# Merging the last two feature groups of an FFN's second product, and a finishing root from a kept eps / r^2

## The chip, the cores and the metric

The kernel runs on one core of one Trainium2 chip (trn2). The metric is the device time of one launch in microseconds; the kernel before was run three times: 2975.94, 2977.49 and 2983.4 us, median 2977.49. One of these executions was profiled, and all rows below are of that one.

## The reference

One layer of a streaming encoder, for 2048 new frames of one stream (the prompt) and 32 frames of a running stream (the sample), 2080 tokens of width 1024, all in float32:

- mixer: RMSNorm, one input projection, eight heads of stick-breaking attention and eight heads of a Mamba-2 scan, both normalised, one output projection; `h = x + RMSNorm(mixer)`;
- FFN: `gu = RMSNorm(h) @ w_up`, whose two halves of 2816 features are the gate and the up branch; the gate goes through a causal convolution over three frames and a GeLU, is multiplied by up, and the result goes through `w_down` (2816 x 1024); `y = h + RMSNorm(f)`, with f the product of `w_down`.

RMSNorm is `x * rsqrt(mean(x*x) + eps) * g` with eps = 1e-6. Outputs are y, the new keys and values, and the states of the scan and of both convolutions.

## The kernel before, in words

Feature-major: 128 channels stand on the partitions, tokens run along the free dimension. Tokens are worked in four blocks (`SBS`, line 37), numbered 0 to 3: three of 512 tokens and one of 544, which is 512 of the prompt and the 32 of the sample. A block of 544 is computed as two tiles of 272 tokens (`tiles_of`, line 58), since one PSUM bank holds 512 columns; the other blocks are one tile.

Products in full precision are made of three fast ones: every operand is held as a high part and a remainder, and `dense` (line 118) issues hi·hi, hi·lo and lo·hi for each 128 rows of the contraction. So a weight tile holds two parts of up to eight 128 x 128 squares (`weight`, line 98), 1024 KB when full. The split is done once, in block 0: load (L107), high part on ScalarE (L108), remainder on GpSimd (L109), store to DRAM (L112). Later blocks load both parts from there with one DMA (L104). Three such tiles rotate (`WBUFS`, line 21), whatever part of a tile is filled.

**The FFN** is `Tail`. `up` (line 979) computes one group of 128 gate features and the 128 up features that belong to them, and leaves the activation as `ah` and `al` (L1033 on ScalarE, then L1034 on GpSimd); there are 22 such features j. `down` (line 1038) multiplies the activations of one entry of `GROUPS` by their rows of `w_down`: for each pair of the eight output squares c it loads a weight tile, accumulates over the n features of the group in one PSUM tile, and adds it to the running sum `f` in SBUF on VectorE (L1065; the first group copies, L1063). With `end` it also squares f (ScalarE L772) and adds up the squares on GpSimd (L773) for the closing norm. Activations have four buffers (line 893).

**Order of the work.** `stream` (line 1094) is the list of steps of one block after its attention: output projection, residual, norm, then for each feature group the `up`s, and one `down` behind the first `up` of the group after. The steps are drawn as filler between the attention instructions of the block that comes next (`fill`, called from `heads`), three matmuls at a time, and TensorE's order is pinned to that list (`pin`). The last two groups' products are not in the list: they are kept as `self.owed` and run in the stream of the block behind, eight steps of them at once (while the norm of the attention output is made) and the others after the residual. Block 3 has no attention behind it: its stream runs alone (`alone`, line 1143), with three PSUM banks for these products and no pinned order, and its owed products close the kernel. There, and only there, the two tiles of 272 tokens are taken one after the other, each with its own loads of the weights, and `finish` (line 1074) closes tile a's norm, adds h and stores y before tile b's in program order. Where nothing is pinned, instructions are put in order at compile time by a list scheduler that simulates the engines; each engine and the SyncE queue of DMAs then run that order.

**Roots.** `rstd_steps` (line 156) turns a sum of squares into reciprocal roots: small matmuls bring the sums into columns (L166), VectorE scales them (L176 or L179), GpSimd raises to the power -0.5 (L184), small matmuls spread the column over partitions again (L195), ScalarE copies it out (L201). `root` makes r, the reciprocal root of the norm ahead of the FFN. r is not applied to the input of the up branch, so f is too small by that factor, and `finish` makes up for it: it calls `rstd_steps` with `of` = the kept column of r.

Of the kernel before, what the change touches and what calls it, by code (L numbers as in the profile page):

```python
# [8 lines left out]
F32 = mybir.dt.float32  # L9
# [3 lines left out]
ALU = mybir.AluOpType  # L13
# [10 lines left out]
P = 128  # L24
# [9 lines left out]
EPS = 1e-6  # L34
# [23 lines left out]
def tiles_of(n):  # L58
    return [(0, n)] if n <= 512 else [(0, n // 2), (n // 2, n)]


class Kernel:
# [93 lines left out]
    def rstd_steps(self, pool, psp, pt, sq, n, width, tag="rstd", out=None, rcol=None, of=None):  # L156


        nc = self.nc
        nb = (n + P - 1) // P  # L160
        nf, e = divmod(n, P)
        ps = psp.tile([P, 512], F32, name=pt)
        for b in range(nb):
            q = min(P, n - b * P)
            for i, t in enumerate(sq):
                nc.tensor.matmul(  # L166
                    ps[:q, b : b + 1], t[:, b * P : b * P + q], self.ones[:, 0:1],
                    start=i == 0, stop=i == len(sq) - 1,
                )
        v = pool.tile([P, 8], F32, name="rn_v") if rcol is None else rcol  # L170
        if e:
            nc.vector.memset(v[:], 1.0)
        if of is None:
            if e:
                nc.vector.tensor_scalar(v[:e, nf:nb], ps[:e, nf:nb], 1.0 / width, EPS, op0=ALU.mult, op1=ALU.add)
            nc.vector.tensor_scalar(v[:, :nf], ps[:, :nf], 1.0 / width, EPS, op0=ALU.mult, op1=ALU.add)  # L176
        else:
            for rows, cols in ((slice(0, P), slice(0, nf)),) + (((slice(0, e), slice(nf, nb)),) if e else ()):
                nc.vector.scalar_tensor_tensor(  # L179
                    v[rows, cols], ps[rows, cols], 1.0 / width, of[rows, cols], op0=ALU.mult, op1=ALU.mult  # L180
                )
            nc.vector.tensor_tensor(v[:, :nb], v[:, :nb], of[:, :nb], op=ALU.mult)
            nc.vector.tensor_scalar(v[:, :nb], v[:, :nb], EPS, 0.0, op0=ALU.add, op1=ALU.add)
        nc.gpsimd.tensor_tensor(v[:, :nb], v[:, :nb], self.mhalf[:, :nb], op=ALU.pow)  # L184
        if of is not None:
            nc.vector.tensor_tensor(v[:, :nb], v[:, :nb], of[:, :nb], op=ALU.mult)
        yield
        r = pool.tile([P, 544], F32, name=tag) if out is None else out
        ps = psp.tile([P, 512], F32, name=pt)
        for b in range(nb):  # L190
            q = min(P, n - b * P)
            if b == 4:
                nc.scalar.copy(r[:, :512], ps[:])
            c0 = b % 4 * P
            nc.tensor.matmul(  # L195
                ps[:, c0 : c0 + q], v[:, b : b + 1].to_broadcast([P, P]), self.ident[:, :q], start=True, stop=True
            )
        if nb == 5:
            nc.scalar.copy(r[:, 512:n], ps[:, : n - 512])
        else:  # L200
            nc.scalar.copy(r[:, :n], ps[:, :n])  # L201
        self.rcol = v
        yield r
# [676 lines left out]
class Tail:  # L880
# [1 line left out]

    GROUPS = [(3 * i, 3) for i in range(6)] + [(18, 2), (20, 2)]

    def __init__(self, kn, att, ctx, pu):
        self.kn, self.att = kn, att
# [149 lines left out]
    def down(self, s, g, acts, tiles, end=False):  # L1038

        kn, nc, att = self.kn, self.kn.nc, self.att  # L1040
        j0, n = self.GROUPS[g]
        first = tiles[0][0] == 0
# [51 lines left out]
    def stream(self, s, cat):  # L1094
        nt = SBS[s][1]
        a, b = (0, nt // 2), (nt // 2, nt)
        owed, self.owed = self.owed or iter(()), None
        yield from islice(owed, 8)
        yield from self.out_units(s, cat, a)
        chain = self.residual(s, a)  # L1100
        for n, _ in enumerate(self.out_units(s, cat, b)):
            yield
            if n % 4 == 0:
                next(chain, None)
        self.root(s, a)
        for _ in self.residual(s, b):
            pass
        self.split(s, a)
        self.split(s, b)
        self.root(s, b)  # L1110
        yield from owed
        done = iter(())
        if s:
            done = (i for h in (0, SBS[s - 1][1] // 2) for i in self.finish(s - 1, h, h + 256, self.f))
        groups = self.GROUPS
        tiles = tiles_of(nt)
        acts = {}
        for g, (j0, n) in enumerate(groups):
            acts[g] = []
            for j in range(j0, j0 + n):  # L1120
                for i, _ in enumerate(self.up(s, j, acts[g])):
                    yield
                    if j and i % 2:
                        next(done, None)
                if j == j0 and g and g < len(groups) - 1:
                    yield from self.down(s, g - 1, acts.pop(g - 1), tiles)
        g = len(groups) - 1

        def last():
            for t in [tiles] if s < NSB - 1 else [[t] for t in tiles]:  # L1130
                for e in range(2):
                    yield from self.down(s, g - 1 + e, acts[g - 1 + e], t, e == 1)
                if s == NSB - 1:
                    for _ in self.finish(s, *t[0], self.f):
                        pass

        self.owed = last()

    def count(self, s):
# [161 lines left out]
```

## Time and profile before

| | |
|---|---|
| runs | 2975.94, 2977.49, 2983.4 us; median 2977.49 |
| profiled execution | 2975.94 us, of which the span from first to last instruction is 2973.7 us |
| TensorE matmuls | 2832.0 us busy (95% of the span), 16175 |
| VectorE | 1576.6 us (53%) |
| ScalarE | 1238.4 us (42%) |
| GpSimd | 1256.1 us (42%) |
| DMA | 571.58 MB, 192 GB/s over the span |
| chain that ended last | TensorE 76%, VectorE 12%, DMA 5% |
| granted TensorE clock | 0.978 of full speed over the span |

In the rows PE is the matmul engine, PEld its weight loads, DVE VectorE, ACT ScalarE, POOL GpSimd, and SPq the SyncE queue that issues nearly all DMAs. Times are microseconds from the first instruction, unless they are marked ns. Block 0's FFN runs from about 900 to 1400 us, block 3 runs alone from about 2447 us, and the closing products begin at about 2917 us. In a line of the timeline the bracket at the end is the time that the engine sat idle ahead of the instruction, and what ended it.

### The profile page before, as it was taken

Reading aid. Unit: us, or ns where it says so; the run is one execution under the profiler, and the core shown is the slowest. Engines: PE = TensorE matmul, PEld = TensorE weight load, DVE = VectorE, ACT = ScalarE, POOL = GpSimd, SP = SyncE. Lnnn points to the kernel's source line nnn. Section 1 sums busy time; section 2 is a strip of 40 time slices with the busy share of each in tenths; the row PEclk is TensorE's granted clock in tenths of the full one; section 3 lists DMA queues with packets and bytes.
Section 4 is the critical chain, followed back from the end, with each engine's and each line's share of the span. In section 5 each row is a group of like instructions: output and inputs, shape, how many; then the busy total and the mean of one; then the engine's idle time right before and its main releaser. Section 6 shows DMA issues by size and latency. Waiting matters only on the chain.

```text
span 2973.7 us, 43439 instructions
## 1 busy us (share of the span) xinstructions
PE 2832.0 (95%) x16175; PEld 2327.7 (78%) x16175; DVE 1576.6 (53%) x2386; ACT 1238.4 (42%) x2514; POOL 1256.1 (42%) x1077
## 2 busy tenths in 40 slices
PE   8999999989989999999999999999999999999996
PEld 6777778866767777887777777867777779899996
DVE  7676676546664544437544445574545544623334
ACT  4344444346665444436433334653444433311111
POOL 3555555344766665547322223462322325411113
PEclk9999999989999999999999999999999999999998
DMA  5545453657666777876654456646444445655555
GB/s 174 178 149 172 149 165 119 177 147 241 211 237 240 263 242 257 280 256 213 207 178 173 161 183 220 199 163 212 161 162 166 149 173 206 223 183 170 178 177 173
DMA packets 234660, 571.58 MB, mean 192 GB/s; under 512 B 49514, under 2 KB 101362, under 8 KB 205906
## 3 DMA queue, kind: packets, MB, share of 16 engines
q1 hardware_dynamic: 234450, 568.81, 57.4%
q8 instruction: 129, 2.11, 0.3%
q14 instruction: 81, 0.66, 0.1%
HBM read 435.22 MB, written 133.50 MB: 191 GB/s over the span
## 4 chain that ended last, share of the span: by engine, by line
PE 76%; DVE 12%; DMA 5%; ACT 2%; issue 2%; POOL 1%; SPq 1%; DVEq 0%; POOLq 0%; ACTq 0%
PE o L124 37%; PE u L124 12%; PE t L124 11%; PE pa L848 4%; PE z L812 4%; PE pt L833 3%; PE o L365 2%; DVE xc L341 2%; DVE prow L662 1%; DMA w<-wS_out 1%; DVE acB L436 1%; DVE x L263 1%; DVE f L1086 1%; DMA acB<-acD 1%; DVE xc L337 1%
## 5 line engine op out<-in xcount | busy, mean ns | idle before, releaser
L124 PE MATMUL o<-xhi,w 128*128 128x512 f32 (+2 forms) x3968 | 1043.3, 346 | 30.9 <-ACT xhi L287 8.0
L124 PEld LDWEIGHTS o<-xhi,w 128*128 128x128 f32 x3968 | 698.2, 192 | 132.1 <-issue 9.3
L124 PE MATMUL o<-xlo,w 128*128 128x512 f32 (+2 forms) x1984 | 684.1, 345 | 4.8 <-DVE xlo L273 3.6
L109 POOL TENSOR_TENSOR w<-wraw,w 128x1024 fp32r<-128x1024 f32 (+2 forms) x156 | 366.6, 2350 | 247.0 <-ACT w L108 219.7
L667 POOL TENSOR_TENSOR beta<-beta,prow 128x512 f32<-128x512 f32 (+3 forms) x256 | 256.7, 1003 | 449.1 <-DVE prow L662 420.7
L124 PEld LDWEIGHTS o<-xlo,w 128*128 128x128 f32 x1984 | 380.7, 192 | 52.8 <-DVE xlo L273 5.3
L124 PE MATMUL u<-xhi,w 128*128 128x512 f32 x1056 | 350.3, 401 | 2.2 <-ACT rstd L201 2.2
L124 PE MATMUL o<-ah,w 128*128 128x512 f32 x992 | 340.7, 404 | 7.5 <-DVE f L1065 7.5
L662 DVE TENSOR_TENSOR_SCAN prow<-gam,prow,z 128x513 f32<-128x513 f32 x192 | 244.9, 1278 | 174.5 <-ACT beta L660 172.7
L1019 POOL TENSOR_TENSOR y<-y,gb 128x512 f32<-128x512 f32 (+1 forms) x88 | 115.6, 1315 | 495.4 <-ACT gb L1018 492.7
L124 PEld LDWEIGHTS u<-xhi,w 128*128 128x128 f32 x1056 | 200.3, 190 | 56.4 <-issue 4.4
L659 ACT ACTIVATE gam<-z 128x512 f32<-128x512 f32 (+2 forms) x320 | 173.4, 542 | 141.0 <-PE z L812 92.4
L124 PEld LDWEIGHTS o<-ah,w 128*128 128x128 f32 x992 | 187.8, 189 | 52.5 <-DVE f L1065 8.9
L836 ACT COPY wt<-pt 128x512 f32<-128x512 f32 (+3 forms) x282 | 148.1, 530 | 178.4 <-PE pt L833 175.8
L124 PE MATMUL u<-xlo,w 128*128 128x512 f32 x528 | 210.7, 399 | 0.0
L108 ACT CAST w<-wraw 128x1024 fp32r<-128x1024 f32 (+2 forms) x156 | 155.2, 995 | 120.0 <-PE o L124 97.1
L1011 DVE SCALAR_TENSOR_TENSOR y<-gb,cv,y 128x512 f32<-128x512 f32 (+1 forms) x176 | 163.1, 927 | 68.9 <-ACT y L1009 66.1
L124 PE MATMUL o<-al,w 128*128 128x512 f32 x496 | 197.0, 397 | 0.0
L124 PE MATMUL t<-xhi,w 128*128 128x272 f32 x960 | 188.2, 292 | 2.9 <-DVE f L1065 2.8
L833 PE MATMUL pt<-ident,beta 128*128 128x128 f32 x1088 | 180.5, 281 | 8.7 <-DVE rn_v L176 3.8
L833 PEld LDWEIGHTS pt<-ident,beta 128*128 128x128 f32 x1088 | 134.3, 144 | 60.6 <-issue 25.1
L662 DVE TENSOR_TENSOR_SCAN prow<-gam,ones,z 128x129 f32<-128x129 f32 (+3 forms) x128 | 112.1, 877 | 126.1 <-ACT beta L660 119.8
(271 smaller groups left out, 4907.9 us busy)
## 6 DMA issues: line engine op xcount, KB each, us to landing
w<-wS_up SPq DMA_DIRECT2D x132, 1024.0 KB, 4.8
w<-wS_dn SPq DMA_DIRECT2D x72, 768.0 KB, 4.8
wS_up<-w SPq DMA_DIRECT2D x44, 1024.0 KB, 4.8
w<-wS_out SPq DMA_DIRECT2D x39, 1024.0 KB, 6.2
wraw<-wup SPq DMA_DIRECT2D x44, 512.0 KB, 5.8
k<-kS SPq DMA_DIRECT2D x80, 256.0 KB, 3.8
wS_dn<-w SPq DMA_DIRECT2D x24, 768.0 KB, 4.5
w<-wS_dn SPq DMA_DIRECT2D x32, 512.0 KB, 4.0
```

Source lines behind the costliest of these rows:

```text
L108: nc.scalar.copy(hi[:, :n, :], raw[:, :n, :])
L109: nc.gpsimd.tensor_tensor(lo[:, :n, :], raw[:, :n, :], hi[:, :n, :].bitcast(F32), op=ALU.subtract)
L124: mm = nc.tensor.matmul(ps[:, : c1 - c0], l[:, k, :], at(r, k0 + k)[:, c0:c1], start=first and i == 0 and k == 0, stop=last and i == 2 and ...
L659: nc.scalar.activation(g[:, c0:512], z, AF.Sigmoid, scale=-0.125)
L662: nc.vector.tensor_tensor_scan(back(pr), back(g), z[:, 0:1].to_broadcast([P, n + 1]), self.kn.ones[:, 0:1] if prev is None else prev, op0= ...
L667: eng.tensor_tensor(b[:, :n], b[:, :n], pr[:, c0 + 1 : 513], op=ALU.mult)
L812: mm = nc.tensor.matmul(z[:, :n], q[:, P * b : P * b + P], k[:, :n], start=e == 0, stop=e == 1 and kc < s)
L833: mm = nc.tensor.transpose(t[:, P * j : P * j + P], w[:, P * j : P * j + P], kn.ident[:])
L836: copy(wt[:, : n // P, P * b : P * b + P], t[:, :n].rearrange("p (i q) -> p i q", q=P))
L848: nc.tensor.matmul(av[DH * (j % 2) : DH * (j % 2) + DH, c0:], v[:, j, :], wt[:, j, c0:], start=kc == s and j < 2, stop=kc == 0 and j > 1,)
L1011: nc.vector.scalar_tensor_tensor(y[:, :W], gb[:, i : i + W], kn.col(wc + i), y[:, :W], op0=ALU.mult, op1=ALU.add)
L1019: nc.gpsimd.tensor_tensor(y[:, :W], y[:, :W], t, op=ALU.mult)
```

## The change

The last two entries of `GROUPS`, (18, 2) and (20, 2), become one, (18, 4). The owed work is then one call of `down` with four features, with `end` set, instead of two with two features each. In `rstd_steps`, a call with `rcol` now keeps eps / r^2 there (one GpSimd multiply of the column ahead of the power) instead of r; a call with `of` adds that kept column in the one VectorE instruction that scales the sum, and the power is then the result, where before it took a product with r, a second product, an addition of eps, the power and a third product. The working column is always a tile of its own, `rn_v`.

```diff
-        v = pool.tile([P, 8], F32, name="rn_v") if rcol is None else rcol
+        v = pool.tile([P, 8], F32, name="rn_v")
         if e:
             nc.vector.memset(v[:], 1.0)
...
+        for rows, cols in ((slice(0, P), slice(0, nf)),) + (((slice(0, e), slice(nf, nb)),) if e else ()):
+            if of is None:
+                nc.vector.tensor_scalar(
+                    v[rows, cols], ps[rows, cols], 1.0 / width, EPS, op0=ALU.mult, op1=ALU.add
+                )
+            else:
                 nc.vector.scalar_tensor_tensor(
-                    v[rows, cols], ps[rows, cols], 1.0 / width, of[rows, cols], op0=ALU.mult, op1=ALU.mult
+                    v[rows, cols], ps[rows, cols], 1.0 / width, of[rows, cols], op0=ALU.mult, op1=ALU.add
                 )
-            nc.vector.tensor_tensor(v[:, :nb], v[:, :nb], of[:, :nb], op=ALU.mult)
-            nc.vector.tensor_scalar(v[:, :nb], v[:, :nb], EPS, 0.0, op0=ALU.add, op1=ALU.add)
+        if rcol is not None:
+            nc.gpsimd.tensor_scalar(rcol[:, :nb], v[:, :nb], EPS, 0.0, op0=ALU.mult, op1=ALU.add)
         nc.gpsimd.tensor_tensor(v[:, :nb], v[:, :nb], self.mhalf[:, :nb], op=ALU.pow)
-        if of is not None:
-            nc.vector.tensor_tensor(v[:, :nb], v[:, :nb], of[:, :nb], op=ALU.mult)
...
-    GROUPS = [(3 * i, 3) for i in range(6)] + [(18, 2), (20, 2)]
+    GROUPS = [(3 * i, 3) for i in range(6)] + [(18, 4)]
...
-                if j == j0 and g and g < len(groups) - 1:
+                if j == j0 and g:
                     yield from self.down(s, g - 1, acts.pop(g - 1), tiles)
...
             for t in [tiles] if s < NSB - 1 else [[t] for t in tiles]:
-                for e in range(2):
-                    yield from self.down(s, g - 1 + e, acts[g - 1 + e], t, e == 1)
+                yield from self.down(s, g, acts[g], t, True)
```

## Rows read from the trace of the kernel before

**Rows 1.** Busy time and granted clock by stretch; the first line names the columns.
```profile
core 0: us, PE busy (x) PEld busy (x) DVE busy (x) ACT busy (x) POOL busy (x), PEclk, DMA share, GB/s
...
2447.00:2917.00 470.00, 460.98 (x3551) 454.33 (x3546) 184.49 (x388) 110.45 (x243) 123.00 (x119) 0.99 0.56 190
2917.00:2974.00 57.00, 33.95 (x217) 31.88 (x215) 29.62 (x70) 8.75 (x20) 23.12 (x26) 0.78 0.61 188
```

**Rows 2.** TensorE's waits, 2917 to 2974: us in total, times, longest.
```profile
PE t L124 <- DMA w<-wS_dn: 4.3, 4, 2.0
PE t L124 <- DVE f L1065: 3.5, 4, 1.5
```

**Rows 3.** Pieces of the chain that ended last: start, us, what, how many.
```profile
1282.92 0.47 PE u L124 x2
...
2911.07 6.03 PE o L124 x48
2917.09 1.52 PE t L124 x12
```

**Rows 4.** Timeline of SyncE's DMA issues from 2905: start, us, count of issues.
```profile
2905.07 6.55 SPq L104 DMA_DIRECT2D w<-wS_dn  x2
...
2917.12 29.78 SPq L104 DMA_DIRECT2D w<-wS_dn  x14
```

**Rows 5.** DMA issues from 2862: count, KB each, median us to landing.
```profile
w<-wS_dn SPq DMA_DIRECT2D x16, 512.0 KB, 4.6
w<-wS_up SPq DMA_DIRECT2D x6, 1024.0 KB, 4.8
```

**Rows 6.** Two stretches of the end, columns as in Rows 1.
```profile
2935.50:2938.90 3.40, 3.40 (x17) 3.40 (x16) 0.88 (x2) 0.00 (x0) 0.00 (x0) 0.50 0.36 128
...
2949.20:2956.00 6.80, 5.93 (x26) 5.93 (x27) 4.96 (x13) 2.44 (x6) 4.73 (x6) 0.50 0.85 281
```

**Rows 7.** GpSimd timeline: remainder of feature 21, blocks 0 and 3.
```profile
1286.37 1.27 POOL L1034 TENSOR_TENSOR al<-y,ah 128x512 fp32r<-128x512 f32 x1 [2.08 <-ACT ah L1033]
...
2920.76 1.35 POOL L1034 TENSOR_TENSOR al<-y,ah 128x544 fp32r<-128x544 f32 x1 [1.72 <-ACT ah L1033]
```

**Rows 8.** TensorE's waits over the whole span, columns as in Rows 2.
```profile
PE o L124 <- DVE f L1065: 7.5, 5, 2.5
PE t L124 <- DVE f L1065: 6.3, 5, 2.8
PE u L195 <- DVE rn_v L186: 6.3, 5, 2.0
...
PE o L124 <- DMA w<-wS_out: 4.7, 2, 3.8
...
PE u L195 <- POOL rcol L184: 3.1, 2, 1.7
PE z L812 <- DVE rn_v L186: 2.3, 2, 1.2
```

**Rows 9.** VectorE timeline, owed products of block 0.
```profile
1370.10 5.73 DVE L946 SCALAR_TENSOR_TENSOR m<-m,cv,rstd 128x256 f32<-128x256 f32 x8 [1.05 <-ACT rstd L201]
1375.75 0.68 DVE L1065 TENSOR_TENSOR f<-o,f 128x512 f32<-128x512 f32 x1
```

**Rows 10.** VectorE timeline at the last root.
```profile
2959.46 0.21 DVE L179 SCALAR_TENSOR_TENSOR rn_v<-u,rcol 128x2 f32<-128x2 f32 x2 [2.25 <-PE u L166]
2959.71 0.16 DVE L182 TENSOR_TENSOR rn_v<-rn_v,rcol 128x3 f32<-128x3 f32 x1
2959.91 0.17 DVE L183 TENSOR_SCALAR rn_v<-rn_v 128x3 f32<-128x3 f32 x1
2961.12 0.16 DVE L186 TENSOR_TENSOR rn_v<-rn_v,rcol 128x3 f32<-128x3 f32 x1 [1.04 <-POOL rn_v L184]
```

**Rows 11.** TensorE timeline at the last root.
```profile
2958.69 0.74 PE L166 MATMUL u<-ones,fsq 128*128 128x1 f32 x6 [1.95 <-POOL fsq L773]
```

**Rows 12.** GpSimd and VectorE groups by shape: count, busy us, mean ns.
```profile
L109 POOL TENSOR_TENSOR w<-wraw,w 128x512 fp32r<-128x512 f32 x8 | 10.6, 1328 | 0.8 <-ACT w L108 0.8
...
L184 POOL TENSOR_TENSOR rcol<-rcol,mhalf 128x2 f32<-128x2 f32 x6 | 4.8, 799 | 6.8 <-DVE rcol L176 5.7 <-DMA v<-vS 1.1
...
L644 POOL MEMSET gam<- 128x1 f32 x3 | 0.2, 99 | 0.0
```

More of the change, by code (lines that the diff above doesn't have):

```diff
@@ L169, in rstd_steps @@
                 )
-        v = pool.tile([P, 8], F32, name="rn_v") if rcol is None else rcol
+        v = pool.tile([P, 8], F32, name="rn_v")
         if e:
             nc.vector.memset(v[:], 1.0)
[L173 to L178, printed above, removed]
+        for rows, cols in ((slice(0, P), slice(0, nf)),) + (((slice(0, e), slice(nf, nb)),) if e else ()):
[4 more added lines that the diff above has]
+            else:
                 nc.vector.scalar_tensor_tensor(
-                    v[rows, cols], ps[rows, cols], 1.0 / width, of[rows, cols], op0=ALU.mult, op1=ALU.mult
+                    v[rows, cols], ps[rows, cols], 1.0 / width, of[rows, cols], op0=ALU.mult, op1=ALU.add
                 )
-            nc.vector.tensor_tensor(v[:, :nb], v[:, :nb], of[:, :nb], op=ALU.mult)
-            nc.vector.tensor_scalar(v[:, :nb], v[:, :nb], EPS, 0.0, op0=ALU.add, op1=ALU.add)
+        if rcol is not None:
+            nc.gpsimd.tensor_scalar(rcol[:, :nb], v[:, :nb], EPS, 0.0, op0=ALU.mult, op1=ALU.add)
         nc.gpsimd.tensor_tensor(v[:, :nb], v[:, :nb], self.mhalf[:, :nb], op=ALU.pow)
-        if of is not None:
-            nc.vector.tensor_tensor(v[:, :nb], v[:, :nb], of[:, :nb], op=ALU.mult)
         yield
```

## The prediction

> **What bounds the kernel now.** I read the busy times by stretch first. In the 470 us in which block 3 runs alone TensorE is busy 461 us at a granted clock of 0.99, and nothing but fewer matmuls would help there; in the last 57 us it is busy 34 us at 0.78 [rows 1]. The change removes no matmul: the owed products are 8 outputs x 4 features x 3 = 96 matmuls per tile in either form. So it can only give back idle TensorE time, and the place to look is that last stretch. Then TensorE's waits there: 4.3 us for weight loads of w_down, 3.5 us for the additions to f [rows 2]. The pace of TensorE at full clock comes from the chain: 48 matmuls of 272 columns in 6.03 us, 0.1256 us each [rows 3]. At that pace the closing products (two tiles, 192 matmuls) need 24.1 us. They begin at 2917.1 [rows 3] and end at 2958.69 - 1.95 = 2956.74, where the idle time ahead of the last root begins [rows 11]: 39.6 us. With 1.5 us for the twelve small matmuls of tile a's root (twice the 0.74 of rows 11) the floor is 25.6 us, and 14.0 us are lost. Part of that is clock: two stretches of 3.4 and 6.8 us, behind waits of TensorE, show a granted clock of 0.50, that is 1.2 instead of 2.4 GHz [rows 6]; at half speed they lose up to 1.7 + 3.4 us.
>
> **Why the weights come late there.** One load of 512 KB serves 12 matmuls, 1.51 us. Three tiles rotate, and a load takes 4.6 us from issue to landing [rows 5], so a tile comes round in 1.51 + 4.6 = 6.1 us and the three of them give one load each 2.04 us. The queue shows 29.78 / 14 = 2.13 us [rows 4]: it is the round trip that sets the pace, not TensorE's 1.51. In the long stretch ahead, one load serves 48 matmuls, and there is no such wait.
>
> **The change part by part** (own time of the profiled execution: 2975.94 us, span 2973.7 and 2.2 around it; 1.55 below the median of the runs).
>
> 1. *Closing products, tail.* Four features fill the tile: 8 loads of 1024 KB in place of 16 of 512. A full load takes 4.8 us [rows 5] and serves 24 matmuls, 3.01 us; the round trip gives one load each (3.01 + 4.8) / 3 = 2.60 us, under 3.01, so TensorE sets the pace and the waits for weights go, with the half clock behind them. What is late next is feature 21: before, the first pass used features 18 and 19 alone, which were long done; now the first output wants 21, whose remainder lands at 2920.76 + 1.35 = 2922.11 [rows 7], 5.0 us after TensorE is free. Nine matmuls (1.1 us) can go ahead, or 27 (3.4 us) if the scheduler starts three outputs in the three banks: idle 1.6 to 3.9 us, I take 2.5. Evacuations halve too, 8 per tile, 3 banks hold 4.5 us of work; tile a's finish puts eight products on VectorE in one go (as the 5.73 us of [rows 9]), so I leave 0.5 us for f, and 0.5 us for a low clock. New tail 25.6 + 3.5 = 29.1 us, gain 10.5. Best 25.6 + 1.6, gain 12.4; worst 25.6 + 3.9, with the 3.5 of f as now and 3.0 of half clock, gain 3.6.
>
> The Trainium skill speaks against the size of this. Its page "DMA: Bandwidth & Descriptors" (section "Anatomy of one DMA — SWDGE (gpsimd) path") fits about 2.0 us plus bytes / 436e3 per DMA, an estimate of 3.2 us for 512 KB and 4.4 for 1 MB; with 3.2 us the round trip would give a load each 1.57 us, close to TensorE's 1.51, and the loads would explain 1 us of the tail. The rows disagree (4.6 us to landing here, loads 2.13 us apart, from SyncE's queue), so I go by them.
>
> 2. *Last root.* On the path that ends last stand L182, L183 and L186, from 2959.71 to 2960.09 and from 2961.12 to 2961.28 [rows 10], 0.16 + 0.17 + 0.16 us and the hops between them: 0.55 us gone, 0.5 to 0.7.
>
> 3. *Owed products of blocks 0 to 2.* TensorE waits 7.5 + 6.3 us for additions to f, of which 3.5 are the tail's: 10.3 us [rows 2, 8]. They arise where VectorE has eight residual products in a row, 5.73 us, with the addition behind them [rows 9], while two PSUM banks hold 6 matmuls each. With 12 per bank the same block of VectorE time is nearly covered, and 24 additions of 0.68 us fall away. Between 0 and 10.3 I take 6.
>
> 4. *Roots inside finish, blocks 0 to 2.* TensorE waits 6.3 + 2.3 us for L186, less 2.0 at the very end: 6.6 us [rows 8]. Without L186 the power on GpSimd releases TensorE; L186 does not queue behind VectorE's other work any more, but the wait for GpSimd stays. Between 0 and 6.6 I take 2.5.
>
> 5. *Root that keeps eps / r^2.* One more GpSimd instruction ahead of the power, eight times. The trace has no such instruction; between the smallest memset, 0.10 us, and the power itself, 0.80 [rows 12], so -0 to +6.4 in sum, and only two of the roots have TensorE waiting for them (3.1 us in two waits [rows 8]): +0.2 to +1.6, I take +1. The others lie beside up products. The queue behind it on GpSimd is the power and the squares; a shift of under 1 us there is hidden by the same products.
>
> 6. *Feature 21 in blocks 0 to 2, and squares that come earlier.* In block 0 TensorE ends the up product at 1283.39 [rows 3], the remainder ends at 1287.64 [rows 7], 4.25 us later; nine matmuls of 0.235 us cover 2.1. Idle 2.1 us, for what is pinned behind it. Behind it a wait for the output projection's weights follows (3.8 of 4.7 us [rows 8]), and one tile of weights less ahead of it lets that load start sooner: the delay may cost nothing or the wait may shrink. Two outputs now also bring their squares into the stretch in which ScalarE and GpSimd make the norm. For three blocks -3.8 to +6.3, I take +2.
>
> 7. *At nothing:* splitting the weights in block 0 (four GpSimd instructions twice as long in place of eight of 1.33 us [rows 12]; the raw loads are as many bytes) and all stores and loads of blocks 0 to 2, hidden by the products of the same stretch; uncovered, one split of a tile, twice 1.33, is the price.
>
> Sum: -10.5 - 0.55 - 6 - 2.5 + 1 + 2 = -16.55 us: 2975.94 - 16.55 = 2959.4 us, against the median 2959.4 + 1.55 = 2961 us.
>
> **The rivals.**
>
> - *All of it.* Every wait for f and L186 goes and the tail meets its best: -12.4 - 0.7 - 10.3 - 3 + 0.2 = -26.2, 2951 us. For it: the waits are named. Against: a wait that goes is often followed by the next in line. 0.12.
> - *The loads were not the limit.* The 2.13 us are the echo of TensorE's other stops; fuller loads give back the 4.3 us booked to them, and the wait for feature 21 takes 3.5 of it: 1 us is left. Then -1 - 0.55 - 6 - 2.5 + 3 = -7, 2970 us. For it: no more than 4.3 us are booked to the loads [rows 2]. Against: the landing time in rows 5. 0.06. (The page's fit, above, would have it so.)
> - *Given back inside.* The tail gains 7, but the new order of the scheduler moves the waits of parts 3 and 4 elsewhere (0 in sum), and parts 5 and 6 cost 1.4 + 3: -7.5 + 4.4 = -3, 2974 us, no difference. For it: these waits are where VectorE's residual products stand, and those stay. 0.15.
> - *Slower: feature 21.* Place: the first output of the owed products in all four blocks. TensorE stands, and then goes at 1.2 GHz as it does behind the waits of rows 6: 2.1 + 3.4 us in each of blocks 0 to 2, 16.5 us; in the tail 3.9 + 3.4 beside the 3.5 for f and the 4.3 for loads, which a late release of the tiles keeps, 15.1 where 14.0 are lost now, +1. Less 8.5 for parts 3 and 4 and plus 1 for part 5 it is +10, 2987 us. It decides from the point where stalls and low clock together pass the 19 us that parts 1 to 4 give. For it: the order is pinned in blocks 0 to 2. Against: a wait of 2.1 us there fits beside the norm, behind which TensorE waits anyway [rows 8]. 0.04.
>
> **How the numbers follow.** Forecast 0.63, at 2961 us, with 2953 to 2968 as its own range; the rivals as above, 0.37. To 2951 on the fast side and 2972 on the slow side the range takes in the full gain, the loads' rival and part of the third; outside is about 0.2. What a measurement tells from no change is about 0.3%, 8.9 us, so faster means under 2968.6: 0.61 of the forecast, 0.12, and 0.05 from the second and third rivals, 0.78. Slower, over 2986.4: 0.05. The remainder 0.17 is the same.
>
> **What would show it.** In the profile after: eight loads of 1024 KB in the tail, about 3 us apart, no wait of TensorE for them, a clock of 1.00 in most of it, closing products done in some 29 us; right at their start a wait for `al` L1034 of 1.6 to 3.9 us. Additions to f behind the first group fall from 7 x 8 outputs x 5 tiles = 280 to 6 x 8 x 5 = 240, and TensorE's wait for them from 13.8 to under 6 us. L182, L183 and L186 are gone and what TensorE waited for them is partly booked to the power. Wrong: loads still more than 3.2 us apart with TensorE waiting for them (part 1), waits for `al` in the owed products of blocks 0 to 2 of more than 2 us each (part 6), or a sum of waits in 1280 to 2917 that is no smaller (parts 3 and 4).

## The result, and the profile after

The changed kernel was slower, not faster: 2985.38 us (median of 22 runs, 2973.27 to 2988.79) against 2978.97 us for the kernel before (22 runs, 2972.66 to 2989.31); ratio 1.002, 95% interval 1.0011 to 1.0028. Forecast was 2961. The profiled execution took 2988.79 us, the longest of its runs, with a span of 2987.0 us; the profiled one of before stood 3 us under its median. So of the 13.3 us between the two spans about half belongs to the executions, and sizes are taken from medians and ratios, places from the traces.

The end of the kernel, where most was forecast, did what it should. Stretches of the kernel after (answers to [rows 1]; the last one begins with the closing products):

```profile
core 0: us, PE busy (x) PEld busy (x) DVE busy (x) ACT busy (x) POOL busy (x), PEclk, DMA share, GB/s
2447.00:2938.00 491.00, 476.70 (x3610) 466.18 (x3609) 185.89 (x383) 115.13 (x252) 125.67 (x124) 0.98 0.55 187
2938.00:2987.00 49.00, 29.64 (x223) 28.20 (x221) 22.64 (x49) 9.28 (x21) 23.03 (x26) 0.87 0.57 197
```

TensorE's waits of the kernel after from 2938 on (answer to [rows 2]):

```profile
PE u L167 <- POOL fsq L772: 3.0, 1, 3.0
PE t L124 <- DVE f L1064: 1.9, 1, 1.9
PE u L194 <- POOL rn_v L185: 1.3, 1, 1.3
PE t L124 <- ACT ah L1032: 1.1, 1, 1.1
PE t L124 <- POOL al L1033: 0.8, 1, 0.8
```

Its SyncE issues there (answer to [rows 4]) and their landing (answer to [rows 5]):

```profile
2926.80 6.35 SPq L104 DMA_DIRECT2D w<-wS_dn  x2
...
2938.85 18.22 SPq L104 DMA_DIRECT2D w<-wS_dn  x6
```

```profile
w<-wS_dn SPq DMA_DIRECT2D x16, 1024.0 KB, 4.9
```

Six loads in 18.22 us are 3.04 us each: the pace is TensorE's 24 matmuls, 3.01 us, and no wait for weights is left. (The 4.9 us are the median of the sixteen such loads of the whole execution, the eight closing ones among them.) The closing products run from 2938.66, their first matmul, to 2969.24, where the idle time ahead of the last root begins: 30.6 us in place of 39.6. But they begin 21.6 us later than the 2917.09 of [rows 3]. Of these, 5.0 us stand ahead of the first output product's copy (782.0 us before, 787.0 after), in work that the change does not touch. Behind it TensorE's idle time grew. From the last up products of block 0 (1280 us) to those of block 2, first in the trace of before and then after, columns as above:

```profile
1280.00:1830.00 550.00, 535.48 (x2630) 417.37 (x2629) 263.50 (x355) 211.32 (x467) 186.55 (x194) 0.98 0.56 193
1830.00:2447.00 617.00, 602.49 (x3039) 460.60 (x3039) 338.82 (x434) 285.87 (x622) 227.26 (x233) 0.99 0.53 177
```

```profile
1280.00:1830.00 550.00, 532.12 (x2586) 411.53 (x2585) 252.69 (x338) 208.99 (x458) 184.79 (x191) 0.98 0.56 193
1830.00:2447.00 617.00, 602.49 (x3052) 461.66 (x3050) 334.13 (x418) 287.31 (x623) 227.60 (x236) 0.99 0.52 176
```

With block 3 up to its closing products (470.00 - 460.98 in [rows 1], 491.00 - 476.70 above) TensorE stands idle for 38 us before and 47 us after. What it waits for over the whole span (answer to [rows 8]) tells part of where that was lost:

```profile
PE z L811 <- DVE prow L661: 24.5, 18, 3.6
PE u L194 <- POOL rn_v L185: 12.4, 6, 4.2
...
PE o L124 <- DVE y L1027: 7.8, 1, 7.8
...
PE o L124 <- DMA w<-wS_out: 4.1, 1, 4.1
...
PE t L124 <- DVE f L1064: 2.1, 2, 1.9
```

and in the trace of before:

```profile
PE z L812 <- DVE prow L662: 16.5, 14, 3.4
...
PE o L124 <- DVE y L1028: 2.7, 1, 2.7
...
PE u L195 <- POOL rn_v L184: 1.4, 1, 1.4
```

The waits for f are nearly gone (13.8 to 2.7 us, 0.6 of it in a row further down). In their place are longer waits for VectorE's scans of the attention, `prow`, and one wait of 7.8 us for an up product, where before took 2.7. The waits for a root did not go: the 12.4 us for the power on GpSimd stand in place of 10.8 (6.3 and 3.1 in [rows 8], and the 1.4).

### The profile page after: what moved, and what is told of

It reads as the page before. It is cut to its first block, busy times and chain, and to the rows that moved or that the text cites. A ratio compares the mean times of both kernels' runs of the same rounds, so it can differ in the third digit from the quotient of the medians.

```text
span 2987.0 us, 43324 instructions
## 1 busy us (share of the span) xinstructions
PE 2837.6 (95%) x16175; PEld 2326.6 (78%) x16175; DVE 1552.6 (52%) x2322; ACT 1239.8 (42%) x2510; POOL 1253.3 (42%) x1081
## 4 chain that ended last, share of the span: by engine, by line
PE 74%; DVE 13%; DMA 5%; issue 3%; ACT 2%; POOL 2%; SPq 1%; DVEq 0%; POOLq 0%; ACTq 0%
PE o L124 36%; PE u L124 12%; PE t L124 10%; PE pa L847 4%; PE z L811 4%; PE pt L832 3%; PE o L364 2%; DVE xc L340 2%; DVE acB L435 1%; DMA acB<-acD 1%; DVE prow L661 1%; DVE xc L336 1%; DVE x L262 1%; DVE xlo L272 1%; DMA w<-wS_out 1%
## 5 line engine op out<-in xcount | busy, mean ns | idle before, releaser
L124 PEld LDWEIGHTS o<-xhi,w 128*128 128x128 f32 x3968 | 699.0, 192 | 138.6 <-issue 13.7
L109 POOL TENSOR_TENSOR w<-wraw,w 128x1024 fp32r<-128x1024 f32 (+1 forms) x152 | 365.7, 2406 | 246.6 <-ACT w L108 221.2
L108 ACT CAST w<-wraw 128x1024 fp32r<-128x1024 f32 (+1 forms) x152 | 154.4, 1016 | 118.6 <-PE o L124 98.1
```

The lines of the kernel that those rows point to most:

```text
L108: nc.scalar.copy(hi[:, :n, :], raw[:, :n, :])
L109: nc.gpsimd.tensor_tensor(lo[:, :n, :], raw[:, :n, :], hi[:, :n, :].bitcast(F32), op=ALU.subtract)
L124: mm = nc.tensor.matmul(ps[:, : c1 - c0], l[:, k, :], at(r, k0 + k)[:, c0:c1], start=first and i == 0 and k == 0, stop=last and i == 2 and ...
```

## Experiments

Each kernel was compared with the kernel before on the same chip; the medians of before were 2978.2 to 2980.2 us. In the diffs `rstd_steps` is meant where nothing else is said.

**The two halves apart.** Merge alone (`GROUPS` ends in (18, 4), old `rstd_steps`):

> One half of the change: GROUPS ends in (18, 4), the roots are those of the kernel before. The tail should show its gain of about 10 us in any theory (8 loads of 1024 KB, about 30 us from the first closing product to the last). Theory A, the merge in blocks 0 to 2 gives it back, since the fuller owed steps move VectorE's and GpSimd's work between the attention's instructions: middle about +16, sum about +6 us, ratio to before 1.002, and a tail that begins some 15 us later than 2917. Theory B, the root gives it back: the middle stays, tail begins within 4 us of 2917, sum -9 to -10, ratio 0.997. Theory C, each edit moves the order of the middle by itself, some 8 us each: sum about -2, ratio 0.9993.

Measured: 2973.54 us, ratio 0.9981 (0.9970 to 0.9991). Root alone (new `rstd_steps`, old `GROUPS`):

> The other half: the finishing root in one step from eps / r^2, GROUPS as before. The tail keeps its 16 loads of 512 KB and its 39.6 us. Theory A (the merge is what costs): the root gives its 0.5 us at the end and up to 2.5 inside, sum -0.5 to -3 us, ratio 0.999 to 1.000. Theory B (the root is what costs; the added GpSimd instruction, and block 2's closing residual products released earlier, ahead of the up products' evictions): +12 to +16 us, ratio 1.004 to 1.0055, and a wait of some 8 us of TensorE for VectorE's up product near 2585. Theory C (both): +5 to +8, ratio 1.002 to 1.003.

Measured: 2985.79 us, ratio 1.0027 (1.0015 to 1.0040). So it is the root that costs, as theory B has it, against my own first guess; but only in kind: B asked for -9 to -10 us of the merge and at least +12 of the root, and -5.0 and +7.3 were measured. The wait near 2585, which I had put to the root, is in the trace of the merge and not of the root. It is told below.

**The merge in the closing products alone.** Block 0 stores the two halves side by side, blocks 1 and 2 load halves, block 3 the whole (entry g + 1 is a further one, (18, 4)):

```diff
...
-                for e in range(2):
-                    yield from self.down(s, g - 1 + e, acts[g - 1 + e], t, e == 1)
+                if s == NSB - 1:
+                    yield from self.down(s, g + 1, acts[g - 1] + acts[g], t, True)
+                else:
+                    for e in range(2):
+                        yield from self.down(s, g - 1 + e, acts[g - 1 + e], t, e == 1)
...
```

> Only block 3's closing products take four features with one load of 1024 KB; blocks 0 to 2 keep (18, 2) and (20, 2) and their roots. All that stands before 2917 us is then the order of the kernel before. Theories A, B and C agree here: tail -9 to -10 us, nothing elsewhere, ratio 0.9965 to 0.997, about 2969 us. Against them theory D, that the tail's gain is not real but taken from the stretch ahead of it (the fuller loads displace others, the up products of features 20 and 21 come later): the tail shortens and begins later by the same, ratio 1.000.

Measured: 2975.79 us, ratio 0.9989 (0.9976 to 1.0002): less than the 9 us expected, and not told apart from no change. Its trace tells why the end gave less. Up to 2900 us VectorE, ScalarE and GpSimd run exactly the instruction sequences of the kernel before (read off both traces: operation, operands, shapes). From the last activation `ah` to the end it takes 47.4 us where before took 53.7: 6.3 us. The loads and f give back their waits as in the changed kernel, but another grows. TensorE's waits from 2917 on:

```profile
PE u L172 <- POOL fsq L779: 5.4, 1, 5.4
PE u L201 <- DVE rn_v L192: 2.0, 1, 2.0
PE t L130 <- ACT ah L1039: 1.1, 1, 1.1
PE t L130 <- POOL al L1040: 0.8, 1, 0.8
PE t L130 <- DMA w<-wS_dn: 0.3, 1, 0.3
```

The squares of f at the end are late by 5.4 us, where [rows 11] had 1.95. VectorE has tile a's eight residual products in one stretch of 5.0 us (2942.8 to 2947.8) ahead of tile b's last three additions to f. That this stretch makes the squares late is read from the order and not shown by a run; the edit meant to test it (under "A miss") changed no order. With the new root beside the merge (the changed kernel, and the next run) the wait is 3.0, and 1.9 us stand as a wait for f instead.

> The closing products as in the run before this one (four features only in block 3), with the finishing root in one step from eps / r^2 everywhere. Theory A: tail -10, root -0.5 to -3, sum -10 to -13, ratio 0.9957 to 0.9967. Theory B: tail -10, root +12 to +16, sum +2 to +6, ratio 1.001 to 1.002. Theory C: -2 to -5, ratio 0.998 to 0.9993.

Measured: 2983.47 us, ratio 1.0015 (1.0005 to 1.0025): theory B again: the root costs 7.7 us beside this merge, 7.3 alone. Beside the whole merge it is more, 2973.5 to 2985.4.

**Which part of the root.** The kept column made by VectorE straight from the sums:

```diff
-            nc.gpsimd.tensor_scalar(rcol[:, :nb], v[:, :nb], EPS, 0.0, op0=ALU.mult, op1=ALU.add)
+            for rows, cols in ((slice(0, P), slice(0, nf)),) + (((slice(0, e), slice(nf, nb)),) if e else ()):
+                nc.vector.tensor_scalar(
+                    rcol[rows, cols], ps[rows, cols], EPS / width, EPS * EPS, op0=ALU.mult, op1=ALU.add
+                )
```

> GROUPS as before; the finishing root in one step, but eps / r^2 is made by VectorE straight from the sums in PSUM (sum x eps / width + eps^2), so that the power on GpSimd has nothing ahead of it. The new root with the GpSimd instruction cost 8 us by itself. Theory R1, it is the GpSimd instruction ahead of the power, for which TensorE waits: then this is -0.5 to -3 us against before, ratio 0.999 to 1.000. Theory R2, it is the shorter finish, which lets the closing residual products of the block before fall elsewhere between the attention's instructions: then the loss stays, +6 to +9 us, ratio 1.002 to 1.003. Theory R3, it is mere chance of the order and of where the clock falls: anything between.

Measured: 2981.85 us, ratio 1.0011 (0.9997 to 1.0024): between R1 and R2, and told apart neither from no change nor from the root with the GpSimd multiply (1.0015 to 1.0040). Theory R3, chance of the order, is not excluded here. With the merge in the closing products:

> Four features in block 3's closing products alone, and the root of e5_root_dve. Against the same kernel with the GpSimd instruction (2983.5 us) and the one with the old root (2975.8): theory R1, 2973 to 2976 us, ratio 0.998 to 0.999; theory R2, 2981 to 2984, ratio 1.001 to 1.002. In either the last root should be 0.5 to 0.7 us shorter than with the old root.

Measured: 2974.73 us, ratio 0.9979 (0.9967 to 0.9991), as R1 has it, and clear of the 1.0015 (1.0005 to 1.0025) with the GpSimd multiply. And the converse, the kernel before with nothing but the GpSimd multiply:

```diff
+        if rcol is not None:
+            scrap = pool.tile([P, 8], F32, name="rn_s")
+            nc.gpsimd.tensor_scalar(scrap[:, :nb], v[:, :nb], EPS, 0.0, op0=ALU.mult, op1=ALU.add)
         nc.gpsimd.tensor_tensor(v[:, :nb], v[:, :nb], self.mhalf[:, :nb], op=ALU.pow)
```

> The kernel before with one thing added: the GpSimd multiply of the column by eps ahead of the power, eight times, into a tile that nothing reads; the finishing root is the old one in five steps. Theory R1 (this instruction is the cost): +6 to +9 us, ratio 1.002 to 1.003. By the prediction's part 5 it would be +0.2 to +1.6, ratio 1.0001 to 1.0005. Theory R2 (the shorter finish is the cost): 0 to +1.6 as well.

Measured: 2989.62 us, ratio 1.0037 (1.0023 to 1.0050). Eight instructions, 2.3 us of GpSimd in sum, cost 10.7 us. The same eight behind the power:

> The kernel before with the dead GpSimd multiply put behind the power instead of ahead of it (it reads r and writes a tile that nothing reads). Ahead of the power it cost 10.7 us, of which TensorE's direct wait for the root's column shows only 0.9 (3.1 to 4.0). Theory P (place: the 0.2 us and the hop ahead of the power delay what waits for the root, and the order follows from that): behind the power it costs 0 to +2 us, ratio 1.000 to 1.0007. Theory Q (any instruction more on GpSimd, wherever it stands, moves the order of the attention's instructions and costs): +6 to +11 us, ratio 1.002 to 1.0037.

Measured: 2976.59 us, ratio 0.9991 (0.9980 to 1.0002): no cost. Theory P. The groups of GpSimd, ahead of the power and then behind it:

```profile
L186 POOL TENSOR_SCALAR rn_s<-rcol 128x2 f32<-128x2 f32 (+1 forms) x8 | 2.3, 285 | 13.2 <-DVE rcol L176 10.7 <-DMA v<-vS 2.3
```

```profile
L187 POOL TENSOR_SCALAR rn_s<-rcol 128x2 f32<-128x2 f32 (+1 forms) x8 | 1.9, 238 | 0.7
```

What the place does: TensorE's waits for the kept column itself rise from 3.1 us to 4.0, no more. But with the multiply behind the power VectorE and ScalarE run exactly the sequences of the kernel before, and GpSimd that sequence and eight more; with it ahead, 39 VectorE, 57 ScalarE and 14 GpSimd instructions stand in another place, around 1350, 1940 to 2030 and 2560 us, and so do over a hundred of TensorE's and 15 DMA issues. (Up to block 3 the pinned products keep their order; TensorE's attention and root matmuls between them do not.) TensorE's waits from block 2's second half of output products to its eighth activation, with the multiply ahead of the power (1890.0 to 2149.4 us):

```profile
PE z L815 <- DVE prow L665: 5.3, 5, 2.8
PE o L124 <- DVE f L1068: 3.7, 2, 3.2
PE u L198 <- DVE rn_v L189: 3.4, 1, 3.4
PE pt L836 <- DVE beta L670: 1.4, 1, 1.4
PE z L815 <- DVE rn_v L189: 1.2, 1, 1.2
PE pa L851 <- ACT wt L839: 1.1, 1, 1.1
```

and behind it (1893.4 to 2148.5 us, 4.3 us shorter):

```profile
PE z L815 <- DVE prow L665: 4.0, 3, 2.8
PE o L124 <- DVE f L1068: 3.5, 2, 1.8
PE u L198 <- DVE rn_v L189: 1.9, 1, 1.9
PE z L815 <- DVE rn_v L189: 1.2, 1, 1.2
PE u L124 <- ACT rstd L204: 1.1, 1, 1.1
PE pt L836 <- POOL beta L670: 1.0, 2, 0.5
```

None of the waits that grew or came new is for the column that was delayed. And the eight instructions are 2.3 us in sum, so their own delay cannot make the 10.7 even if TensorE waited for all of it. A run with the delay in place and the old order held fixed was not made.

**The change as it is, with that one instruction moved.** Merge 2973.5 and root 2985.8 alone would add to +2.3 us, the change has +6. So the whole change was run with the multiply behind the power (which then writes to a tile of its own, `rn_p`):

```diff
+        m = v
         if rcol is not None:
-            nc.gpsimd.tensor_scalar(rcol[:, :nb], v[:, :nb], EPS, 0.0, op0=ALU.mult, op1=ALU.add)
-        nc.gpsimd.tensor_tensor(v[:, :nb], v[:, :nb], self.mhalf[:, :nb], op=ALU.pow)
+            v = pool.tile([P, 8], F32, name="rn_p")
+        nc.gpsimd.tensor_tensor(v[:, :nb], m[:, :nb], self.mhalf[:, :nb], op=ALU.pow)
+        if rcol is not None:
+            nc.gpsimd.tensor_scalar(rcol[:, :nb], m[:, :nb], EPS, 0.0, op0=ALU.mult, op1=ALU.add)
```

> The changed kernel, all of it, with the GpSimd multiply that keeps eps / r^2 put behind the power (the power writes to a tile of its own). Placed ahead of the power in the kernel before, the same multiply cost 10.7 us, behind it nothing. Theory P (the place ahead of the power is what turns the change into a loss): 2973 to 2977 us, ratio 0.998 to 0.999, some 8 to 12 us under the changed kernel's 2985.4. Theory X (merge and one-step root collide by themselves): 2982 to 2988, ratio 1.001 to 1.003.

Measured: 2970.43 us, ratio 0.9978 (0.9969 to 0.9987), a little beyond theory P's range. And with VectorE making the column (the edit of e5_root_dve):

> The changed kernel, all of it, with eps / r^2 made by VectorE from the sums in PSUM and no GpSimd multiply. Theory P: 2970 to 2975 us, ratio 0.997 to 0.9985 (the merge alone was 2973.5, the kernel with two passes kept in block 2 and this root 2964.0, of which some 5 to 6 us are block 2's passes). Theory X: 2982 to 2988, ratio 1.001 to 1.003.

Measured: 2970.21 us, ratio 0.9975 (0.9964 to 0.9987). Theory P in kind in both. One instruction of some 0.2 us, eight times, decides between a loss of 6 us and a gain of 8. The stretch from block 1's second half of output products to block 2's eighth activation, first in the changed kernel and then with the multiply moved (columns as in [rows 1]):

```profile
1333.60:2155.10 821.50, 791.98 (x3942) 610.78 (x3941) 425.01 (x559) 353.98 (x782) 305.14 (x325) 0.99 0.55 188
```

```profile
1331.60:2139.10 807.50, 788.16 (x3940) 606.68 (x3939) 429.57 (x559) 352.57 (x783) 307.11 (x325) 0.99 0.56 191
```

14.0 us, where the two spans differ by 13.7: 10.2 of it idle TensorE, 3.8 longer busy time. The granted clock is 0.50 for 23.9 us of the first stretch and 17.1 us of the second, which at half speed is up to 3.4 us. One of the waits shows how an order costs. The changed kernel's GpSimd, around block 0's finish:

```profile
1445.58 1.29 POOL L1033 TENSOR_TENSOR al<-y,ah 128x512 fp32r<-128x512 f32 x1
1450.45 0.72 POOL L1089 TENSOR_TENSOR f<-f,xr 128x256 f32<-128x256 f32 x1 [3.58 <-DMA xr<-hS]
1451.13 0.70 POOL L185 TENSOR_TENSOR rn_v<-rn_v,mhalf 128x2 f32<-128x2 f32 x1
```

and with the multiply moved:

```profile
1437.33 0.92 POOL L1092 TENSOR_TENSOR f<-f,xr 128x256 f32<-128x256 f32 x1
1439.39 0.71 POOL L186 TENSOR_TENSOR rn_v<-rn_v,mhalf 128x2 f32<-128x2 f32 x1 [1.15 <-DVE rn_v L180]
1444.18 0.73 POOL L1092 TENSOR_TENSOR f<-f,xr 128x256 f32<-128x256 f32 x1 [4.08 <-DMA xr<-hS]
```

In the first the power of the finishing root stands behind an addition that waits 3.58 us for its load of h, and TensorE waits 4.2 us for that root; in the second it stands ahead of the addition, and TensorE does not wait.

**Where the merge itself loses.** Block 2's owed products, which open block 3, were put back to two passes; blocks 0, 1 and 3 stay merged, roots as before (entries g + 1 and g + 2 are further ones, (18, 2) and (20, 2), whose weights are halves of the stored tile):

```diff
...
+                if s == NSB - 2:
+                    for e in range(2):
+                        yield from self.down(s, g + 1 + e, acts[g][2 * e : 2 * e + 2], t, e == 1)
+                else:
+                    yield from self.down(s, g, acts[g], t, True)
...
```

> The old roots; four features merged in the owed products of blocks 0 and 1 and in the closing products, while block 2's owed products, which run at the start of block 3, keep two passes of two features (from slices of the same stored weights). The merged kernel lost 8.8 us in the stretch of block 3 that begins with its last output products, 6.6 of them one wait of TensorE for VectorE's up product, and got 2.8 back behind it. If the merge of block 2's owed products is the cause: that wait goes, -5 to -6 us against the merged kernel (2973.5), so about 2968 us, ratio 0.996 to 0.9967. If the wait comes from the blocks before or from the closing products' loads, it stays and the ratio is 0.998.

Measured: 2968.83 us, ratio 0.9959 (0.9943 to 0.9975), as expected. The long wait is an order as well. VectorE in the changed kernel:

```profile
2576.94 6.82 DVE L1085 SCALAR_TENSOR_TENSOR f<-f,cv,rstd 128x256 f32<-128x256 f32 x8
2583.68 0.94 DVE L1089 TENSOR_TENSOR f<-f,xr 128x256 f32<-128x256 f32 x1
2584.54 0.14 DVE L180 SCALAR_TENSOR_TENSOR rn_v<-u,rcol 128x2 f32<-128x2 f32 x1
2584.61 0.74 DVE L1027 TENSOR_TENSOR y<-o,y 128x272 f32<-128x272 f32 x2
```

and with two passes in block 2:

```profile
2564.55 0.76 DVE L1031 TENSOR_TENSOR y<-o,y 128x272 f32<-128x272 f32 x2
2565.22 0.18 DVE L1033 TENSOR_TENSOR y<-o,y 128x32 f32<-128x32 f32 x1
2565.81 5.81 DVE L1089 SCALAR_TENSOR_TENSOR f<-f,cv,rstd 128x256 f32<-128x256 f32 x8 [0.40 <-ACT rstd L204]
```

The up product's multiply, which frees a PSUM bank, stands behind block 2's eight residual products in the one and ahead of them in the other; 7.8 us of TensorE against 2.7. (The merge alone, with the same roots as the second, has 6.6.) Both mends together:

> Four features merged in the owed products of blocks 0 and 1 and in the closing products, two passes in block 2's, with the one-step root whose eps / r^2 VectorE makes from PSUM. Merged this way with the old root it was 2968.8 us (ratio 0.9959). If the new root without the GpSimd instruction is worth its 0.55 us at the end and costs nothing inside: 2967 to 2969, ratio 0.9954 to 0.996. If it keeps the +3 that it showed alone (1.0011): 2971 to 2973, ratio 0.997 to 0.9978.

Measured: 2963.99 us, ratio 0.9946 (0.9932 to 0.9959): under both expected ranges, the fastest of all, and faster than both kernels. The next wait in line shows here: from 2480 to 2640 us no wait for the up product's multiply is left, but TensorE waits 6.0 us, once, for a load of up weights.

**A miss.** To take away the late squares, the steps of `finish` for tile a were drawn between tile b's products, alone and with the mended root:

```diff
...
+                fin = self.finish(s, *ta, self.f)
+                next(fin)
+                for i, _ in enumerate(self.down(s, g, acts[g], [tb], True)):
+                    if i > 5 and i % 3 == 0:
+                        next(fin, None)
+                    yield
...
```

> Merged but for block 2, old root, and one more edit in the closing products: the steps of finish for tile a are drawn one by one between the products of tile b, where they stood all ahead of them in program order. With the merge TensorE waits 5.4 us for the squares of f at the end (2.0 before), and the eight residual products of tile a stand on VectorE in one stretch of 5.0 us ahead of tile b's last three additions to f. If that stretch is the cause, the wait shrinks to 2 to 3 us and the time to 2965 to 2967 (ratio 0.995 to 0.9956). If GpSimd's own chain of squares is the limit, the wait stays near 5 and the time near 2969.

Measured: 2970.19 us, ratio 0.9969 (0.9957 to 0.9982).

> The two edits of the runs before this one together: tile a's finish spread over tile b's products, and the one-step root with eps / r^2 from VectorE. If both add up: 2964 to 2967 us, ratio 0.9945 to 0.9957. If the root keeps its +3: 2968 to 2970, ratio 0.996 to 0.997.

Measured: 2964.97 us, ratio 0.9953 (0.9938 to 0.9967). The traces show why nothing came of it: VectorE, ScalarE and GpSimd run the very sequences of the two kernels without this edit. Where nothing is pinned the list scheduler does not take the program's order as it stands; the wait for the squares stays 5.4 us with the old root and 3.0 with the new. As repetitions the pairs are of use: 2968.8 and 2970.2, 2964.0 and 2965.0, so in these two pairs a median of six to eight runs moved by 1.0 and 1.4 us by itself.

## Why the prediction was wrong

1. *Closing products*: right in kind. Forecast 39.6 to 29.1, measured 30.6. Waits for weights 4.3 to 0 as said; feature 21 costs 1.9 (1.1 for `ah`, 0.8 for `al`), inside the 1.6 to 3.9, with 27 matmuls ahead of it; f 1.9 instead of 0.5; the squares of f, which I had at no loss, 3.0 in place of 1.95 (they stand behind the 30.6). By itself, with the old root, the merge of the closing products gives 6.3 us of the trace, not 10.5, for the squares are then 5.4 late. The loads were the limit, as the landing times said. The 4.6 us of a half load belong to the closing products, though: over the whole trace of before the 32 half loads of these weights take 4.0 us (median). By the Trainium skill's page "DMA: Bandwidth & Descriptors" (section "Anatomy of one DMA — SWDGE (gpsimd) path") 1 MB would be an estimate of 4.4 us. The row has 4.9, for loads from SyncE's queue and not from GpSimd's.

2. *Last root*: right. From the first small matmul to the copy 2958.69 to 2962.90 before, 2972.27 to 2975.82 after: 4.21 to 3.55, 0.66 us for 0.55.

3. *Waits for f*: they went further than I took (13.8 to 2.7), and of the 6 us no gain is shown. The merge alone and the kernel that merges only at the end have medians of 2973.5 and 2975.8, 0.9981 and 0.9989 with intervals that overlap. In their traces, from the first output product's copy (at 785 us in both) to the last `ah`, the merge inside is 2.4 us longer: what f gave is taken by `prow` (24.2 us against 18.4) and by the one wait for y (6.6 against 2.7). The sign that the prediction set for this part came as well: in the changed kernel TensorE's idle time from 1280 us to the closing products is no smaller, 47 us against 38.

4. *Roots inside finish*: -2.5 forecast, not shown. In the changed kernel two of these roots still cost 4.2 and 2.2 us, now as waits for the power; with the multiply behind the power TensorE waits for none of them inside, so the wait went further than I took. But the time hardly followed: 0.9981 for the merge alone, 0.9978 and 0.9975 with the mended root, and the intervals overlap. Beside other forms of the merge the root with VectorE's column gives 0.0010 to 0.0016 of the time, alone it costs 0.0011; in each of these pairs the intervals overlap too.

5. **The step that failed**: "One more GpSimd instruction ahead of the power ... I take +1", with at most 1.6. The direct wait was well bounded (0.9 us in the run with the multiply alone). Wrong was that this is all: the shift changed the order in which the other engines' instructions stand, and that costs 10.7 us in the kernel before and 1.0020 - 0.9978 of the time, 12.5 us, in the changed one. "A shift of under 1 us there is hidden by the same products" holds of the pinned products, which keep their order up to block 3, not of the attention matmuls between them and of the queues that feed them. Nor did anything in the prediction price an order: part 5 was added up from one instruction's duration and its direct wait.

6. *Feature 21 in blocks 0 to 2*: it costs 0.9 us of wait for `al`, and the wait of 3.8 us for the output projection's weights behind block 0 is gone, better than the +2 taken. (In the changed kernel a wait of 4.1 us for such weights stands further on, at 1356 us; with the multiply moved it is 0.3.) What I did not have is block 2: its owed products open block 3, where nothing is pinned, and merged they cost the wait for y. Two passes there are worth 0.9981 - 0.9959 with the old root and 0.9975 - 0.9946 with the mended one, 6.6 and 8.6 us (4.7 and 6.2 by the medians). With the mended root that is not the one wait alone: a wait of 5.0 us for y goes, and the one for up weights grows from 1.9 to 6.0.

Steps 5 and 6 are where the loss arose: with both mended the kernel gains 0.0054 of 2980.2 us, 16.2 us, where 16.55 were forecast. That the two numbers meet is in part luck, for steps 1, 3 and 4 gave less than they were taken for, and a block 2 in two passes is not the kernel that was forecast. Of the rivals, "given back inside" named the mechanism (the scheduler's new order moves the waits elsewhere) and gave it 0 in sum; it was worth 12.5 us, more than the 9.0 of the closing products. The slower rival put the loss at feature 21, and there it was not.

That the place of one instruction is the cause is shown by the pairs in which it alone was moved. That it works through the order follows from the sizes, since the instruction's own delay is too small. How much of the 12.5 us is any single wait is not shown: the traces differ in hundreds of places (247 VectorE instructions between the changed kernel and the one with the multiply moved), and the clock behind the waits adds to it.

## What to carry to other kernels

Where a list scheduler fixes the order at compile time, price a small edit on a chain that many things wait for by the order it may change as well as by its own wait: put new work off the chain and see whether the engines' sequences stay as they were. Behind the power the extra multiply left them alone and cost nothing; off the chain is no promise, for the root with its column straight from the sums changed the order too (20 ScalarE instructions against the kernel before) and alone was no faster. Test the parts of a change apart: here the merge by itself was worth some 5 us, and one misplaced instruction beside it made a loss of 6. And look at what the change does in the part that is not pinned before booking a wait as gone; the next instruction in the queue inherits the place.

## What the runs showed of the hardware that was not expected

The same wait can leave TensorE's clock up in one execution and down in another. At block 3's first root TensorE waits 1.37 us, once, with the merge in the closing products alone, and 1.37 us, once, with two passes in block 2 and the old root. In the 6.8 us behind, the first runs 56 matmuls at a granted clock of 1.00 and the second 34 at 0.50. In two other kernels the waits there are 1.37 and 0.15 us (before) and 1.38 and 0.52 us (the new root alone); the 6.8 us behind are, first in the kernel before and then with the new root:

```profile
2456.50:2463.30 6.80, 6.78 (x55) 6.74 (x56) 2.45 (x7) 1.96 (x5) 4.13 (x5) 1.00 1.02 428
```

```profile
2471.30:2478.10 6.80, 6.80 (x34) 6.77 (x33) 1.43 (x4) 1.17 (x3) 4.14 (x5) 0.50 1.01 424
```

55 matmuls at 2.4 GHz against 34 at 1.2: some 3 us, between two traces that differ by 0.4 us of waiting. The stretch ahead of the first output product's copy, the same work in all these kernels, took 782.0 to 792.0 us in the sixteen traces. A single profile is no measure of a change of 0.2%.
